# First-group transposes on TensorE, and the DRAM round trip split into a write and a later read, both on SyncE

## The chip, the core and the metric

The kernel runs on one core of a Trainium2 chip. Its engines are TensorE (PE: matrix products and transposes by a product with the identity), VectorE (DVE), ScalarE (ACT), GpSimd (POOL) and SyncE (SP, which only issues transfers here). Each engine works through its own instructions in order; an instruction waits until the semaphores of what it needs are reached, and what stands behind it on its engine waits too. The metric is the device time of one execution in microseconds (us), lower is better.

## The reference, cut to what matters

Two models are chained on an input of 256 rows x 1024, all in float32. The first has four layers, each a mixer (retention, conformer convolution, short convolution, retention) and an MLP. The second has two layers of FFN, token mix (RWKV-7, gated linear attention and gated delta net side by side), FFN and a small gated projection (PLE).

```python
def squared_relu_mlp(x, w1, w2):                 # w1 1024x4096, w2 4096x1024
    return jnp.square(jax.nn.relu(x @ w1)) @ w2

def _swiglu(x, w1, w3, w2):                      # w1, w3 1024x2816, w2 2816x1024
    return (jax.nn.silu(x @ w1) * (x @ w3)) @ w2

# first block, per layer i
x = x + rms_norm(mixer(rms_norm(x, g0)), g1)
x = x + rms_norm(squared_relu_mlp(rms_norm(x, g2), mlp_w1[i], mlp_w2[i]), g3)
# second block, per layer i
x = layer_norm(a * x + 0.5 * _swiglu(x, first FFN's weights))
x = layer_norm(a * x + token_mixing(x, ...))
x = layer_norm(a * x + 0.5 * _swiglu(x, second FFN's weights))
x = layer_norm(a * x + sigmoid(x @ ple_w_gate[i]) * (p[i] @ ple_w_proj[i]))
```

In the token mix, the RWKV branch forms a decay from `tanh(w_lo) @ w2`; `tanh(w_lo)` is the tile `tw` below.

## The kernel before

**Products.** Each float32 operand is split into a high and a low part: `t2h`/`t2l` for the activations (cast on ACT, L351; subtraction on DVE, L352), `wh`/`wl` for the weights (L223, L224; the trace prints the low ones as `whl` and `whxl`). `mm3` (L59) then runs three matmuls, high x high, low weight x high, high weight x low, per 128 x 512 tile of the result. A unit is one 128 x 1024 or 128 x 2 x 512 piece of weights: six matmuls per half of the rows.

**Halves.** The 256 rows are two halves of 128, h0 and h1. `drive` walks through a stage's units; h1 uses a unit five units after h0 (`PACE`), so a weight is loaded and split once. Weights are loaded by SP ahead of their use (`load_unit`, L201) into a few buffers `raw` and `rawx`, cast and subtracted some units ahead (`split_unit`), and released when h1 is done.

**MLP and FFN.** `mlp` takes the hidden width of 4096 in eight groups of 512: four `w1` units per group, then relu (ACT) and the square (DVE), then four `w2` units that add into the accumulators `acc`. `ffn` has eleven groups of 256 with four `f1` and two `f2` units, and silu (ACT) and a product `glu` (DVE) between. The order is w1(0), w1(1), w2(0), w1(2), w2(1) and so on, so each group has one w1 group of time between its activation and its use as the left operand.

**The transpose between.** The activation must be transposed to be the left operand. For all groups but the last, `tr_dma` does this without PE: DVE transposes 32 x 32 blocks into `tz` (L369), POOL issues the write of `tz` to a DRAM tile `td` (L371), and SP issues four reads back into `ty` in the other block order (L375), placed behind the last weight load asked for (`issue_after(s.last_load)`). At k == 4 of the next w1 group, `split_late` casts `ty` to `t2h` and subtracts for `t2l`, placed behind the last weight cast. The last group (7 of the MLP, 10 of the FFN) is transposed on PE with the identity (`tr`, L66 in the trace, into `tp`), since no w1 group is left to hide a trip behind.

**What sets the order.** A scheduler orders each engine's instructions from the program, with its own model of durations, and the `issue_after` edges bind it. In the token-mix phases `side_step` weaves the three branches' chains between the units: a chain yields a number, and is continued when the builder's clock has advanced by so much. `H_W` is the number the RWKV chain yields between `tw` and its use (L1215).

Of the kernel before, what the change touches and what calls it, by code (L numbers as in the profile page):

```python
# [28 lines left out]
SIDE_1 = 1.6  # L29
H_L = 8.0  # L30
H_P = 9.0
H_W = 4.0
H_C = 5.0
H_E = 4.0
LATENCY = 3.5
# [15 lines left out]
class Builder:  # L51
# [309 lines left out]
            s.nc.tensor.transpose(tp[:, j, :], src[:, j * 128:(j + 1) * 128], s.ident)  # L361
        return tp

    def tr_dma(s, src, n):


        nc = s.nc
        z = s.B2((128, 4, n, 32), "tz")
        nc.vector.transpose(z, src.rearrange("p (c a j) -> p a c j", a=4, j=32))  # L369
        d = s.dram.tile([128, 4, n * 32], F32, tag=f"td{n}", bufs=4, name="td")  # L370
        nc.gpsimd.dma_start(d, z.rearrange("p a c j -> p a (c j)"))  # L371
        y = s.B2((128, 4, n, 32), "ty")
        with s.tc.issue_after(s.last_load):
            for a in range(4):
                nc.sync.dma_start(y[32 * a:32 * a + 32].rearrange("i b c j -> i b (c j)"),  # L375
                                  d.rearrange("(b i) a x -> a i b x", b=4)[a])
        return y.rearrange("p b c j -> p c b j")

    def split_late(s, src):
# [90 lines left out]
    def mlp(s, h, lhs, rin):  # L470
        nc = s.nc
        out = [s.acc(), s.acc()]
        r = {}

        def w1(g):
            mm = s.mmb()
            for k in range(0, 8, 2):
                W = yield "w1"
                if k == 4 and g:
                    at[g - 1] = [s.split_late(r.pop(g - 1))]  # L480
                for kk in range(2):
                    s.mm3(lhs, k + kk, W, [(mm, kk * 512, 512, k + kk == 0, k + kk == 7)])
            a = s.B2(name="relu")
            nc.scalar.activation(a, mm, AF.Relu, scale=rin)
            a2 = s.B2(name="relu2")
            nc.vector.tensor_tensor(a2, a, a, op=ALU.mult)

            r[g] = s.tr_dma(a2, 4) if g < 7 else a2

        at = {}  # L490
        yield from w1(0)
        for g in range(8):
            if g < 7:
                yield from w1(g + 1)
            for k in range(4):
                W = yield "w2"
                if g == 6 and k == 1:
                    at[7] = [s.tr_split(r.pop(7))]
                s.mm3(at[g], k, W, [(out[c], c * 512, 512, g == 0 and k == 0, g == 7 and k == 3) for c in range(2)])
        return out  # L500

# [370 lines left out]
    def ffn(s, h, lhs):  # L872
        nc = s.nc
        out = [s.acc(), s.acc()]
        r = {}

        def w1(g):
            mm = s.mmb()
            for k in range(0, 8, 2):
                W = yield "f1"  # L880
                if k == 4 and g:
                    at[g - 1] = [s.split_late(r.pop(g - 1))]
                for kk in range(2):
                    s.mm3(lhs, k + kk, W, [(mm, kk * 512, 512, k + kk == 0, k + kk == 7)])
            a = s.B2((128, 256), "silu")
            nc.scalar.activation(a, mm[:, 0:256], AF.Silu)
            b = s.B2((128, 256), "glu")
            nc.vector.tensor_tensor(b, a, mm[:, 256:512], op=ALU.mult)
            r[g] = s.tr_dma(b, 2) if g < 10 else b

        at = {}
        yield from w1(0)
        for g in range(11):
            if g < 10:
                yield from w1(g + 1)
            for k in range(2):
                W = yield "f2"
                if g == 9 and k == 1:
                    at[10] = [s.split(s.tr(r.pop(10), 2)[:, 0:2, :])]
                s.mm3(at[g], k, W, [(out[c], c * 512, 512, g == 0 and k == 0, g == 10 and k == 1) for c in range(2)])  # L900
        return out

# [268 lines left out]
    def rwkv(s, h, i, q):  # L1171
# [24 lines left out]
        def need(name):  # L1196
            if (name, i, h) not in sh:
                yield name, i, h
            if h and name != "lo" and ("halo", name, i) not in sh:
                yield "halo", name, i  # L1200
            return sh[name, i, h]
# [12 lines left out]
        k = yield from need("rk")  # L1214
        yield H_W  # L1215
        pw, pa = s.mmb((128, 4, 128)), s.mmb((128, 4, 128))
# [679 lines left out]
```

## Time and profile before

| what | value |
|---|---|
| three runs | 3037.0, 3037.02, 3039.89 us, median 3037.02 |
| profiled execution | 3039.6 us, span of the core 3037.8 us, mean granted TensorE clock 0.987 |
| busy, share of the span | PE 96%, PE weight loads 77%, DVE 66%, ACT 50%, POOL 10% |
| transfers | 548.95 MB, 181 GB/s on average |

The stages lie in this order in the span (us, rounded, from the timeline): retention to 223, MLP to 409, conformer to 547, MLP to 735, short convolution to 830, MLP to 1010, retention to 1218, MLP to 1400; then FFN to 1600, mix to 1976, FFN to 2180, PLE to 2208, FFN to 2417, mix to 2795, FFN to 3000, PLE to the end.

In the rows below, a timeline row has the start, the duration, the engine, the line, the operation and `output<-input`, and in brackets how long the engine was idle before it and what released it. A row of waits has the total, the number and the longest. A row of issues has the number, KB each and the median us from issue to landing. A row of windows has for each engine the busy time and (instructions), then the granted clock, the busy share of the DMA engines and GB/s. Matmuls are pipelined: their starts tell the pace, their ends are modelled.

### The profile page before, as it was taken

The page shows a single profiled execution, that of the slowest core. Times are in us where ns is not written, and L with a number is a line of the kernel's source. Part 1 is how long each engine was busy: PE and PEld are TensorE (multiplying, and loading weights), DVE is VectorE, ACT ScalarE, POOL GpSimd, SP SyncE. Part 2 cuts the span into 40 slices and gives each one's busy share as a digit, 9 for nine tenths or more (in the row PEclk, how much of TensorE's full clock was granted, in tenths as well). Part 3 has the DMA queues.
Part 4 walks back from the last instruction along what each step waited for, and adds up shares of the span by engine and source line. Part 5 has one row for each costly group of instructions (what it writes and reads, how often), then busy time and mean ns, then how long its engine had stood idle before and what let it go on. Part 6 is the DMA issues. An engine that isn't in the chain of part 4 may idle for free. (4 is left out here: it accounts for less than half of the span.)

```text
span 3037.8 us, 49444 instructions
## 1 busy us (share of the span) xinstructions
PE 2922.3 (96%) x18650; PEld 2342.2 (77%) x18650; DVE 1993.3 (66%) x3175; ACT 1522.0 (50%) x2348; POOL 289.1 (10%) x488
## 2 busy tenths in 40 slices
PE   8999998999999999999999999989999999999998
PEld 6777877788778878787877777868777777777786
DVE  7566678666766756665567766665665676667556
ACT  4454554555544535544447664444444486654443
POOL 0000024100000000120001000000011100000000
PEclk9999999999999999999999999999999999999999
DMA  7466752576677645786766233477667643335673
GB/s 237 154 186 225 245 160 71 184 251 209 187 237 242 191 155 179 230 262 196 221 187 176 79 112 106 132 218 230 197 196 224 179 131 100 104 112 155 210 234 123
DMA packets 342991, 548.95 MB, mean 181 GB/s; under 512 B 76757, under 2 KB 205985, under 8 KB 342752
## 3 DMA queue, kind: packets, MB, share of 16 engines
q1 hardware_dynamic: 325760, 496.02, 53.3%
q0 software_dynamic: 16416, 47.67, 4.7%
q8 instruction: 147, 2.41, 0.3%
q10 hardware_dynamic: 576, 2.10, 0.2%
q14 instruction: 92, 0.75, 0.1%
HBM read 519.45 MB, written 26.21 MB: 180 GB/s over the span
## 5 line engine op out<-in xcount | busy, mean ns | idle before, releaser
L59 PE MATMUL acc<-wh,t2h 128*128 128x512 f32 (+1 forms) x1512 | 618.5, 409 | 37.4 <-ACT t2h L351 35.7
L59 PE MATMUL acc<-whl,t2h 128*128 128x512 f32 (+1 forms) x1512 | 597.9, 396 | 0.4 <-DVE whl L224 0.4
L224 DVE TENSOR_TENSOR whl<-raw,wh 128x1024 fp32r<-128x1024 f32 x341 | 414.7, 1218 | 250.1 <-ACT wh L223 244.1
L223 ACT CAST wh<-raw 128x1024 fp32r<-128x1024 f32 x341 | 356.8, 1046 | 392.5 <-PE acc L59 259.7
L59 PE MATMUL acc<-wh,t2l 128*128 128x512 f32 (+1 forms) x1512 | 511.6, 395 | 3.1 <-DVE t2l L352 3.1
L224 DVE TENSOR_TENSOR whxl<-raw,whx 128x1024 fp32r<-128x1024 f32 x272 | 329.8, 1214 | 224.5 <-ACT whx L223 220.0
L223 ACT CAST whx<-raw 128x1024 fp32r<-128x1024 f32 x272 | 284.4, 1047 | 300.5 <-PE acc L59 136.8
L59 PEld LDWEIGHTS acc<-wh,t2h 128*128 128x128 f32 x1512 | 287.7, 190 | 115.4 <-ACT t2h L351 49.0
L59 PE MATMUL acc<-whx,t2h 128*128 128x512 f32 (+1 forms) x856 | 348.2, 407 | 4.7 <-ACT t2h L351 4.5
L59 PE MATMUL acc<-whxl,t2h 128*128 128x512 f32 (+1 forms) x856 | 339.1, 396 | 0.0
L59 PEld LDWEIGHTS acc<-wh,t2l 128*128 128x128 f32 x1512 | 285.8, 190 | 67.7 <-DVE t2l L352 6.7
L59 PEld LDWEIGHTS acc<-whl,t2h 128*128 128x128 f32 x1512 | 287.8, 190 | 54.6 <-issue 1.0
L59 PE MATMUL mm<-whx,t2h 128*128 128x512 f32 x800 | 312.9, 392 | 5.9 <-ACT whx L223 5.3
L59 PE MATMUL mm<-whx,t2l 128*128 128x512 f32 x800 | 311.6, 390 | 0.7 <-DVE t2l L352 0.7
L59 PE MATMUL mm<-whxl,t2h 128*128 128x512 f32 x800 | 311.8, 390 | 0.4 <-DVE whxl L224 0.4
L59 PE MATMUL acc<-whx,t2l 128*128 128x512 f32 (+1 forms) x856 | 285.4, 395 | 5.4 <-DVE t2l L352 5.3
L224 DVE TENSOR_TENSOR whxl<-rawx,whx 128x1024 fp32r<-128x1024 f32 x142 | 173.1, 1220 | 126.7 <-ACT whx L223 123.5
L224 DVE TENSOR_TENSOR whl<-rawx,wh 128x1024 fp32r<-128x1024 f32 x145 | 177.2, 1223 | 118.7 <-ACT wh L223 112.1
L223 ACT CAST wh<-rawx 128x1024 fp32r<-128x1024 f32 x145 | 152.4, 1051 | 162.2 <-PE acc L59 106.9
L223 ACT CAST whx<-rawx 128x1024 fp32r<-128x1024 f32 x142 | 148.8, 1049 | 167.5 <-PE mm L59 90.4
L59 PEld LDWEIGHTS acc<-whx,t2h 128*128 128x128 f32 x856 | 163.1, 191 | 43.5 <-ACT t2h L351 7.5
L59 PEld LDWEIGHTS acc<-whx,t2l 128*128 128x128 f32 x856 | 162.8, 191 | 42.0 <-DVE t2l L352 7.0
(618 smaller groups left out, 4190.8 us busy)
## 6 DMA issues: line engine op xcount, KB each, us to landing
raw<-in_mlp_w SPq DMA_DIRECT2D x153, 512.0 KB, 4.6
raw<-in_w_in SPq DMA_DIRECT2D x128, 512.0 KB, 3.6
raw<-in_ffn_w SPq DMA_DIRECT2D x216, 256.0 KB, 3.8
rawx<-in_mlp_w SPq DMA_DIRECT2D x103, 512.0 KB, 4.6
rawx<-in_ffn_w SPq DMA_DIRECT2D x136, 256.0 KB, 3.9
raw<-in_ret_w_in SPq DMA_DIRECT2D x58, 512.0 KB, 4.1
raw<-in_ffn_w SPq DMA_DIRECT2D x53, 512.0 KB, 4.5
rawx<-in_ret_w_in SPq DMA_DIRECT2D x38, 512.0 KB, 4.3
```

The lines of the kernel that those rows point to most:

```text
L59: r = m0(out, a, b, **k)
L223: c = nc.scalar.copy(wh[:, 0:n], r[:, 0:n])
L224: nc.vector.tensor_tensor(wl[:, 0:n], r[:, 0:n], wh[:, 0:n].bitcast(F32), op=ALU.subtract)
```

## The change

It has four parts. Group 0 of every MLP and FFN is transposed on PE, at k == 4 of w1(1). For the other groups but the last, `tr_dma` is split: `tr_out` does the DVE transpose and issues the write to DRAM, now on SP behind the last weight load asked for, and `tr_in` issues the four reads, written at k == 1 of the previous group's second projection, again behind the last weight load then. POOL issues none of these writes any more. And `H_W` goes from 4 to 8.

```diff
-H_W = 4.0
+H_W = 8.0
...
-    def tr_dma(s, src, n):
+    def tr_out(s, src, n):
         nc = s.nc
         z = s.B2((128, 4, n, 32), "tz")
         nc.vector.transpose(z, src.rearrange("p (c a j) -> p a c j", a=4, j=32))
         d = s.dram.tile([128, 4, n * 32], F32, tag=f"td{n}", bufs=4, name="td")
-        nc.gpsimd.dma_start(d, z.rearrange("p a c j -> p a (c j)"))
+        with s.tc.issue_after(s.last_load):
+            nc.sync.dma_start(d, z.rearrange("p a c j -> p a (c j)"))
+        return d, n
+
+    def tr_in(s, dn):
+        d, n = dn
         y = s.B2((128, 4, n, 32), "ty")
         with s.tc.issue_after(s.last_load):
             for a in range(4):
-                nc.sync.dma_start(y[32 * a:32 * a + 32].rearrange("i b c j -> i b (c j)"),
-                                  d.rearrange("(b i) a x -> a i b x", b=4)[a])
+                s.nc.sync.dma_start(y[32 * a:32 * a + 32].rearrange("i b c j -> i b (c j)"),
+                                    d.rearrange("(b i) a x -> a i b x", b=4)[a])
         return y.rearrange("p b c j -> p c b j")
...
     def mlp(s, h, lhs, rin):
-                if k == 4 and g:
+                if k == 4 and g > 1:
                     at[g - 1] = [s.split_late(r.pop(g - 1))]
+                if k == 4 and g == 1:
+                    at[0] = [s.tr_split(r.pop(0))]
...
-            r[g] = s.tr_dma(a2, 4) if g < 7 else a2
+            r[g] = s.tr_out(a2, 4) if 0 < g < 7 else a2
...
                 if g == 6 and k == 1:
                     at[7] = [s.tr_split(r.pop(7))]
+                elif g < 6 and k == 1:
+                    r[g + 1] = s.tr_in(r[g + 1])
...
     def ffn(s, h, lhs):
-                if k == 4 and g:
+                if k == 4 and g > 1:
                     at[g - 1] = [s.split_late(r.pop(g - 1))]
+                if k == 4 and g == 1:
+                    at[0] = [s.split(s.tr(r.pop(0), 2)[:, 0:2, :])]
...
-            r[g] = s.tr_dma(b, 2) if g < 10 else b
+            r[g] = s.tr_out(b, 2) if 0 < g < 10 else b
...
                 if g == 9 and k == 1:
                     at[10] = [s.split(s.tr(r.pop(10), 2)[:, 0:2, :])]
+                elif g < 9 and k == 1:
+                    r[g + 1] = s.tr_in(r[g + 1])
```

How this moves instructions, at three places.

**SP in the first FFN.** `in_ffn_w_2` are weight loads, `td` the write to DRAM (L372 in the changed kernel), `ty` the reads (L375 before, L382 in the changed kernel). Before:

```order
L201 DMA raw<-in_ffn_w_2 128x2x256 x2
L375 DMA ty<-td 32x4x64 x4
L201 DMA raw<-in_ffn_w_2 128x2x256 x2
L201 DMA raw<-in_ffn_w_2 128x1024
L201 DMA rawx<-in_ffn_w_2 128x1024
L201 DMA rawx<-in_ffn_w_2 128x2x256
L375 DMA ty<-td 32x4x64 x4
```

In the changed kernel:

```order
L201 DMA raw<-in_ffn_w_2 128x1024
L372 DMA td<-tz 128x256
L201 DMA rawx<-in_ffn_w_2 128x1024
L201 DMA rawx<-in_ffn_w_2 128x2x256 x2
L382 DMA ty<-td 32x4x64 x4
L201 DMA raw<-in_ffn_w_2 128x2x256 x6
L372 DMA td<-tz 128x256
L201 DMA rawx<-in_ffn_w_2 128x1024
L372 DMA td<-tz 128x256
L201 DMA rawx<-in_ffn_w_2 128x1024
L382 DMA ty<-td 32x4x64 x4
```

Each write now stands in SP's order, and between it and its own reads stand some weight loads (none to three of them, or the other half's write). In the MLPs it is a write, two loads, the reads, then again. The sequence of the 1124 weight loads themselves is the same in both.

**PE in the first MLP, group 0 of h0.** `mm` is the first projection, `acc` the second. Before, the second projection begins:

```order
L59 MATMUL mm<-whl,t2h 128x512
L59 MATMUL mm<-wh,t2l 128x512
L59 MATMUL acc<-wh,t2h 128x512
L59 MATMUL acc<-whl,t2h 128x512
L59 MATMUL acc<-wh,t2h 128x512
```

In the changed kernel the transposes come first, 21 matmuls of the first projection follow, and then the second begins as before:

```order
L59 MATMUL mm<-wh,t2h 128x512
L59 MATMUL mm<-whl,t2h 128x512
L59 MATMUL mm<-wh,t2l 128x512
L66 MATMUL tp<-ident,relu_1941 128x128 x4
L59 MATMUL mm<-whx,t2h 128x512
L59 MATMUL mm<-whxl,t2h 128x512
```

The 16 first groups bring 8 x 4 transposes in the MLPs and 8 x 2 in the FFNs; the DRAM round trips go from 136 to 120.

**PE in the first mix.** `lo` is the input of the RWKV chain's short vectors, whose transposes lead to `tw`; `w2a` are the small weights applied to `tw`. Before, 24 matmuls with weights stand between the transposes of h0's `lo` and the first use of `tw`, the last of them here:

```order
L59 MATMUL acc<-wh,t2h 128x512
L59 MATMUL acc<-whl,t2h 128x512
L59 MATMUL acc<-wh,t2l 128x512
L59 MATMUL mm<-tw,w2a_10927 128x128 x4
L59 MATMUL tp<-shd,w2a_10927 128x128 x4
```

In the changed kernel there are 42, and the other half's `lo` is transposed before them:

```order
L66 MATMUL mm<-ident,lo 128x128 x2
L66 MATMUL mm<-ident,lo 32x128
L59 MATMUL acc<-wh,t2h 128x512
L59 MATMUL acc<-whl,t2h 128x512
L59 MATMUL acc<-wh,t2l 128x512
L59 MATMUL acc<-wh,t2h 128x512
L59 MATMUL acc<-whl,t2h 128x512
L59 MATMUL acc<-wh,t2l 128x512
L59 MATMUL tp<-tw,w2a_10890 128x128 x4
```

The steps that follow in the chain, and the other two branches' steps woven among them, take other places in both mixes as a result.

## The prediction

> **What bounds the kernel now.** I read the page's busy rows first, then PE's waits, then the timeline at the longest of them.
>
> ```profile
> PE 2922.3 (96%) x18650; PEld 2342.2 (77%) x18650; DVE 1993.3 (66%) x3175; ACT 1522.0 (50%) x2348; POOL 289.1 (10%) x488
> PE acc L59 <- ACT t2h L351: 40.2, 27, 3.4
> PE acc L59 <- DVE t2l L352: 8.4, 7, 2.6
> L59 PE MATMUL acc<-wh,t2h 128*128 128x512 f32 x1496 | 613.7, 410 | 37.4 <-ACT t2h L351 35.7 <-DVE rb L563 1.0 <-ACT sg L616 0.5
> ```
>
> TensorE (PE) sets the end: 2922 of the 3037.8 us span. An edit gains only what lies in PE's remaining 115 us, or in a slow PE clock. The largest single wait there is the second projection (accumulator `acc`) waiting for ScalarE's cast `t2h` of the transposed activation: 40.2 us in 27 waits (columns: total, times, longest). One of them, in the first MLP's first group:
>
> ```profile
> 232.72 0.71 DVE L369 STREAM_TRANSPOSE tz<-relu 128x512 f32<-128x512 f32 x1
> 233.72 0.55 POOL L371 DMA_DIRECT2D td<-tz  x1 [0.81 <-DVE tz L369]
> 238.32 1.75 SPq L375 DMA_DIRECT2D ty<-td  x4
> 241.96 0.62 ACT L351 CAST t2h<-ty 128x512 fp32r<-128x512 f32 x1 [2.17 <-DMA ty<-td]
> 240.31 0.39 PE L59 MATMUL mm<-wh,t2l 128*128 128x512 f32 x1
> 242.63 0.50 PE L59 MATMUL acc<-wh,t2h 128*128 128x512 f32 x1 [1.93 <-ACT t2h L351]
> 242.96 0.39 PE L59 MATMUL acc<-whl,t2h 128*128 128x512 f32 x1
> 243.19 0.39 PE L59 MATMUL acc<-wh,t2h 128*128 128x512 f32 x1
> ```
>
> Start, duration, engine; in brackets the idle time and its releaser. DVE's block transpose starts at 232.72, the write and read-back through DRAM last until 241.96, and PE stands for 1.93. Matmuls otherwise start 0.227 apart, so the first one's 0.33 and the modelled end (0.39 against 0.227) add 0.27 to each stall. The trip takes about 9 us; the first group has the work of one group to hide it, every later group more.
>
> Long stalls also slow what follows:
>
> ```profile
> 2017.81 0.79 PE L59 MATMUL acc<-wh,t2h 128*128 128x512 f32 x1 [3.04 <-ACT t2h L351]
> 2023.94 0.40 PE L59 MATMUL acc<-wh,t2h 128*128 128x512 f32 x1
> 2017.10:2023.90 6.80, 6.09 (x14) 4.79 (x15) 2.77 (x5) 2.04 (x4) 0.54 (x1) 0.50 0.53 185
> 2024.00:2031.00 7.00, 7.00 (x32) 5.58 (x31) 3.23 (x4) 2.68 (x4) 0.54 (x1) 1.00 0.64 187
> 262.60:266.10 3.50, 3.50 (x10) 2.68 (x10) 1.88 (x4) 1.08 (x2) 0.54 (x1) 0.51 0.22 80
> 569.80:576.70 6.90, 6.25 (x15) 4.90 (x16) 4.16 (x5) 3.18 (x4) 0.58 (x1) 0.51 0.74 258
> 2232.10:2239.00 6.90, 6.08 (x14) 4.84 (x15) 1.96 (x6) 0.97 (x3) 1.09 (x2) 0.51 0.92 290
> 2836.30:2843.10 6.80, 5.64 (x13) 4.46 (x14) 2.76 (x5) 2.04 (x4) 0.54 (x1) 0.50 0.64 213
> ```
>
> In the window rows the third number from the end is the granted clock. After the 3.04 us stall it is 0.50 for about 7 us, and 14 matmuls take 6.13 us instead of 3.2.
>
> **The change, part by part.**
>
> *Term A, first groups go to PE.* There are 16 first groups (8 stages, two halves); 13 stall: 1.93, 2.17, 3.17, 1.17, 1.15, 0.85 and 1.46 in the four MLPs, 2.32, 1.73, 3.04, 3.19, 1.67 and 3.39 in the FFNs. Sum 27.2. Restarts: 13 x 0.27 = 3.5. Five of them are followed by a half-clock window (the rows above): 6.13 - 14 x 0.227 - 0.27 = 2.7 for the one shown, 11.7 for the five together with each's own rows. After the change the trip to DRAM is gone there, and in the new order PE has 21 or more matmuls (4.8 us) between the transposes and their use, against 1.3 us for cast and subtraction. A = 42.4 gained; nothing else is late at these places, since weights are cast before PE asks for them there.
>
> *Term B, the transposes on PE.* Last groups already do it:
>
> ```profile
> 379.12 0.62 PE L59 MATMUL acc<-wh,t2l 128*128 128x512 f32 x2
> 379.58 0.60 PE L66 MATMUL tp<-ident,relu 128*128 128x128 f32 x4
> 379.94 0.48 PE L59 MATMUL acc<-wh,t2h 128*128 128x512 f32 x1
> 380.25 0.40 PE L59 MATMUL acc<-whl,t2h 128*128 128x512 f32 x1
> PE tp L66 <- DVE glu L888: 1.0, 2, 0.7
> ```
>
> Four transposes hold the stream 0.36, and the next step is 0.31 instead of 0.227: 0.45. Two cost about 0.24. MLPs 8 x 0.45, FFNs 8 x 0.24: 5.5 lost. Existing ones wait little for their input (1.0 us, twice); up to 0.7 for each of 16, 11 us, is the upper bound.
>
> *Term C, H_W.* Its longer wait moves side-chain work in both mix phases:
>
> ```profile
> PE tp L59 <- ACT tw L1213: 3.5, 1, 3.5
> PE mm L59 <- ACT tw L1213: 1.8, 1, 1.8
> PE mm L59 <- DVE yn L607: 2.1, 6, 0.6
> PE tp L66 <- DVE x L924: 4.4, 5, 2.4
> ```
>
> In before, PE runs 24 weight matmuls (5.4 us) between the chain's transposes and the use of `tw`, and stands 1.8 and 3.5 us; now 42 matmuls (9.5 us) stand there. Gone: 5.3, restarts 0.5 and 0.8 of a half clock after the longer one: 6.6. But everything behind it in the chain moves too, and in the new order a few dependent steps of the other chains stand with nothing between. The trace has no row for them; the nearest are short side waits (`yn`, 0.6 at most) and 2.4 at most for `x`. Bounds: from no new wait (+6.6) to eight of 1.5 (-5.4). I take +4, because most distances stay long, and -1.5 for the last small stage, where a transpose now follows its layer norm more closely.
>
> *Term D, the write leaves POOL.*
>
> ```profile
> L371 POOL DMA_DIRECT2D td<-tz x136 | 74.0, 544 | 1111.5 <-DVE tz L369 1065.5 <-DVE whl L224 17.2 <-issue 13.4
> 2306.41 0.45 DVE L369 STREAM_TRANSPOSE tz<-glu 128x256 f32<-128x256 f32 x1
> 2312.97 0.56 POOL L371 DMA_DIRECT2D td<-tz  x1
> 2322.35 0.50 PE L59 MATMUL acc<-wh,t2h 128*128 128x512 f32 x1 [2.77 <-ACT t2h L351]
> ```
>
> POOL mostly idles for `tz`, so its 74 us are worth nothing. But in the third FFN one write queues 6.1 us behind parameter loads on POOL, and PE later stands 2.77. On SP it does not: +3.0 with the restart.
>
> *Term E, writes and reads in SP's queue.* The nearest rows (issues with KB and median us to landing; the extremes are `ty`'s), and the tightest later group:
>
> ```profile
> SPq L375 <- DMA td<-tz: 303.8, 123, 8.8
> td<-tz POOLq DMA_DIRECT2D x80, 128.0 KB, 3.6
> ty<-td SPq DMA_DIRECT2D x320, 32.0 KB, 2.2
> rawx<-in_ffn_w SPq DMA_DIRECT2D x136, 256.0 KB, 3.9
> DMA to landing us min/median/max: 1.6/2.2/7.3
> 1493.92 0.45 DVE L369 STREAM_TRANSPOSE tz<-glu 128x256 f32<-128x256 f32 x1
> 1497.95 2.89 SPq L375 DMA_DIRECT2D ty<-td  x4
> 1502.32 0.41 ACT L351 CAST t2h<-ty 128x256 fp32r<-128x256 f32 x1 [1.69 <-DMA ty<-td]
> 1504.81 0.39 PE L59 MATMUL acc<-whx,t2h 128*128 128x512 f32 x1
> ```
>
> The write now waits on SP for `tz`, with weight loads queued behind; but SP already stood 303.8 us for `td` in before and the weights never came late, and the new wait ends sooner. Then come one or two loads and the four reads. The trace shows no `td` on SP. Lower bound: the 2.2 of a small read there; upper: the 3.9 of a load. I take 2.5, nearer the read, since 128 KB is small. Trip after `tz`, with L for the landing: 0.3 + L + 0.9 (two loads) + 1.75 (four issues) + 2.2 = 5.2 + L, so 7.7, against 1502.3 - 1494.4 = 7.9 from `tz`'s end to the cast here. This group's PE use came 2.1 us after its cast, in most 3 to 5. Cost: nothing while L is under about 4.8, plus 1 us for one late group at the end of the third FFN, where a long load run precedes the write.
>
> The Trainium skill, "DMA: Bandwidth & Descriptors", section "Queues, rings and completion order", says that on each DMA engine the descriptors of one issuing row are consumed in ring order, and that rows are served round-robin. By that a write on SP's row lands behind the loads ahead of it, where POOL's row let it pass. That speaks against the change; no row here shows it, and it would make L that of a load.
>
> **Sum**: 42.4 - 5.5 + 4 - 1.5 + 3.0 - 1 = 41.4. The profiled execution's own time was 3039.6, so 2998.2 for one like it; it lies 2.6 above the runs' median of 3037.0, from which the sum gives 2995.6. I predict **2996 us**.
>
> **Rivals.**
>
> 1. *The half clock is not the stalls' doing.* It also appears elsewhere, and of two stalls of about 2 us one (2.17) is followed by it and one (1.93) not. If the windows merely move to the next pause, 11.7 is not gained: 3008. Against it: all five follow a stall over 2 us within a microsecond. By the Trainium skill, "TensorE: Matmul & The Clock Gate", Part 1, half rate comes after an idle window of about 3.4 us; none of these stalls is that long, yet the granted clock fell, so the rows already go beyond the rule.
>
> 2. *Side chains pay for H_W.* New waits at Term C's lower bound: 9.4 less than I take, and as much again if the chains end the phase late: 3005 to 3015.
>
> 3. *The new transposes wait for their input*, so that the change does not do what it says. 16 x 0.7 = 11: 3007. Against: the row of `glu`, two waits only.
>
> 4. *FFN reads come late, some.* L near 5.5: the 36 first-half groups lose about 0.5 each with restart: 3014.
>
> 5. *Slower side: the same place, L of 7.* Weight loads saturate the queue and each write lands behind two of them. Then the trip is 12.2, 4.3 more than in before; less the usual slack of 3, plus 0.27, each of the 36 groups stalls 1.6: 57 lost, 3053. It decides from about 4.8 and eats the whole gain near 6.4. For it: a read took 7.3 at worst, and the DMA share (second number from the end in the window rows) is 0.92 in one FFN window. Against: medians of 3.6 and 2.2, and shares of 0.53 and 0.64 in two others.
>
> **How the numbers follow.** Forecast (2988 to 3002): 0.60. Rival 1: 0.08, 2: 0.10, 3: 0.06, 4: 0.09, 5: 0.07. This kernel's runs cannot tell less than 0.2% (6 us) from no change. Forecast and rivals 1 to 3 are faster (0.84), 4 mostly (0.05 of 0.09); no change 0.05; slower 0.06. The range leaves out rival 5 and part of 2 and of 4: 2985 to 3016.
>
> **What would show it.** Right: PE's wait on `t2h` falls from 40 us to under 8 and its first-group places vanish from the timeline; windows of 0.5 clock at the five stages are gone; `tp<-ident,relu` doubles to 64 and PE busy rises by about 3 to 5 less the clock's 12; `tw` leaves PE's waits; `td` on SP lands in 2 to 3 us and PE shows no wait for `t2h` in FFN groups 1 to 9. Wrong: `td` landing above 4.8 us, PE waiting for `ty` through the FFNs, casts `wh` waiting for `raw`, or new side waits in the mix phases.

## The result, and the profile after

| kernel | runs | median us | ratio to before, 95% interval |
|---|---|---|---|
| before | 3035.63 to 3039.89 | 3037.01 | |
| after | 2991.6 to 2998.18 | 2993.52 | 0.9858 [0.9841, 0.9875] |

The changed kernel is faster by 1.4%. Its profiled execution took 2998.18 us with a span of 2996.4, so it is 41.4 shorter than that of before (3037.8). First the page's busy row, PE's wait for `t2h`, the transposes by tile, and the issues with their median time to landing:

```profile
PE 2914.0 (97%) x18698; PEld 2341.8 (78%) x18698; DVE 1983.5 (66%) x3159; ACT 1522.3 (51%) x2348; POOL 213.1 (7%) x352
PE acc L59 <- ACT t2h L351: 9.9, 12, 2.2
L66 PE MATMUL tp<-ident,relu 128*128 128x128 f32 x64 | 9.6, 272 | 0.0
L66 PE MATMUL tp<-ident,glu 128*128 128x128 f32 x32 | 6.1, 273 | 0.3 <-DVE glu L901 0.3
td<-tz SPq DMA_DIRECT2D x48, 256.0 KB, 3.2
ty<-td SPq DMA_DIRECT2D x192, 64.0 KB, 5.1
td<-tz SPq DMA_DIRECT2D x72, 128.0 KB, 2.4
ty<-td SPq DMA_DIRECT2D x288, 32.0 KB, 2.9
```

PE's wait for `t2h` fell from 40.2 us in 27 waits to 9.9 in 12; no first group is among them. The two longest, 2.25 and 2.02 us in the conformer, stood in before at the same length.

The write lands 2.4 us (FFN) and 3.2 us (MLP) after its issue on SP, sooner than the 3.6 and 3.7 that it took on POOL. The reads take longer: 5.1 in the MLPs, 2.9 in the FFNs, against 2.3 and 2.2 in before.

What a first group's transposes now cost is seen in the timeline of the first MLP. Starts lie 0.23 apart, but 0.36 and 0.32 around the four transposes:

```profile
237.06 0.60 PE L66 MATMUL tp<-ident,relu 128*128 128x128 f32 x4
237.42 0.48 PE L59 MATMUL mm<-whx,t2h 128*128 128x512 f32 x1
237.74 0.39 PE L59 MATMUL mm<-whxl,t2h 128*128 128x512 f32 x1
```

Two whole stages in windows, the first MLP and the second FFN, first in before, then in after (the length stands behind the bounds, the granted clock third from the end):

```profile
232.20:407.00 174.80, 170.70 (x753) 140.14 (x752) 107.95 (x117) 87.92 (x107) 11.46 (x21) 0.99 0.70 226
1987.00:2165.20 178.20, 173.42 (x751) 140.62 (x750) 102.91 (x131) 78.88 (x107) 11.11 (x21) 0.98 0.73 223
```

```profile
233.80:403.40 169.60, 169.59 (x760) 140.04 (x759) 106.60 (x115) 88.06 (x107) 3.88 (x7) 1.00 0.78 227
1971.20:2145.90 174.70, 173.19 (x761) 140.26 (x759) 104.19 (x131) 80.64 (x110) 0.72 (x2) 1.00 0.77 228
```

The MLP is now busy from end to end (169.59 of 169.60) at full clock. The FFN has its full clock back too, but keeps 1.5 us of idle PE: not all is right there.

Where the 41.4 lie (us from the first transpose on PE of a stage to that of the next, profiled executions; the token mixes begin with their second half's, the PLEs count with the FFN ahead of them, the last one to its last matmul):

| stages | before | after | gain |
|---|---|---|---|
| MLP 1 to 4 | 185.5, 186.1, 181.6, 183.4 | 180.3, 180.6, 179.8, 179.7 | 5.2, 5.5, 1.8, 3.8: 16.2 |
| FFN 1 to 4 | 200.6, 232.0, 209.2, 231.3 | 197.3, 222.8, 202.9, 223.3 | 3.3, 9.2, 6.3, 8.0: 26.8 |
| token mix 1 and 2 | 375.4, 378.3 | 378.5, 375.7 | -3.1, 2.7: -0.4 |
| all else | | | -1.3, of it -2.0 in the first retention |

The 2.0 of the first retention are not the change's: a stretch at half clock stands there at 22 us, which the changed kernel's other profiled execution, after_again below, doesn't have (211.8 us there, 211.2 in before, 213.2 here).

### The profile page after: what moved, and what is told of

The parts are those of the page before. It is cut to its first block, busy times and chain, and to the rows that moved or that the text cites. A ratio compares the mean times of both kernels' runs of the same rounds, so it can differ in the third digit from the quotient of the medians.

```text
span 2996.4 us, 49205 instructions
## 1 busy us (share of the span) xinstructions
PE 2914.0 (97%) x18698; PEld 2341.8 (78%) x18698; DVE 1983.5 (66%) x3159; ACT 1522.3 (51%) x2348; POOL 213.1 (7%) x352
## 5 line engine op out<-in xcount | busy, mean ns | idle before, releaser
L59 PE MATMUL acc<-wh,t2h 128*128 128x512 f32 (+1 forms) x1512 | 611.6, 405 | 10.9 <-ACT t2h L351 8.5
```

The costliest lines, as they stand in the source:

```text
L59: r = m0(out, a, b, **k)
```

## The gain that nobody asked for, and the loss

Two places in the FFNs go otherwise than the prediction has it; both are a matter of one engine's order, and the experiments below turn on them.

**At the end of the second and fourth FFN** (the ones ahead of a PLE) PE waits for the last subtraction. VectorE's and PE's timeline there in before, with a window behind the pause, and then in after:

```profile
2179.91 1.41 DVE L922 SCALAR_TENSOR_TENSOR z<-z,mv,v 128x512 f32<-128x512 f32 x2
2181.24 1.41 DVE L924 SCALAR_TENSOR_TENSOR x<-z,rstd,v 128x512 f32<-128x512 f32 x2
2182.56 1.29 DVE L352 TENSOR_TENSOR t2l<-tp,t2h 128x512 fp32r<-128x512 f32 x2
2183.30 0.73 PE L59 MATMUL acc<-whx,t2l 128*128 128x512 f32 x2 [2.65 <-DVE t2l L352]
2183.00:2191.00 8.00, 7.70 (x27) 6.20 (x28) 3.12 (x4) 0.00 (x0) 0.48 (x1) 0.79 0.88 294
```

```profile
2159.72 0.64 DVE L352 TENSOR_TENSOR t2l<-tp,t2h 128x512 fp32r<-128x512 f32 x1
2160.34 1.41 DVE L937 SCALAR_TENSOR_TENSOR z<-z,mv,v 128x512 f32<-128x512 f32 x2
2160.42 0.74 PE L59 MATMUL acc<-whx,t2l 128*128 128x512 f32 x2 [0.31 <-DVE var L644]
```

In before the subtraction stood behind four operations of the layer norm; in after it stands ahead of them. PE's pause fell from 2.65 to 0.31, and the half-clock stretch behind it (0.79 on average over 8 us, that is 3.4 us at half, which costs 1.6) is gone. That is 2.65 - 0.31 + 1.6 = 3.9 us, and 7.9 with the fourth FFN's, where 2.65 became 0.34. Nothing in the diff names these instructions; the scheduler put them in another order once the stage's work had changed.

**In the later groups of each FFN** some casts of the transposed activation come late. ScalarE in after, first half of the first FFN, group 8, with the reads' row (four of the five are this group's; the reads issued from 1527.7 to 1529.1 land at most 3.3 later) and what PE does:

```profile
L382 SPq DMA_DIRECT2D ty<-td x5: 376/430/432, 1527.2 to 1529.1; - x5
DMA to landing us min/median/max: 1.7/2.0/3.3
1535.90 1.05 ACT L223 CAST wh<-raw 128x1024 fp32r<-128x1024 f32 x1 [1.66 <-PE acc L59]
1536.86 0.40 ACT L351 CAST t2h<-ty 128x256 fp32r<-128x256 f32 x1
1536.56 0.61 PE L59 MATMUL acc<-wh,t2l 128*128 128x512 f32 x2
1537.30 0.50 PE L59 MATMUL acc<-wh,t2h 128*128 128x512 f32 x1
1537.64 0.40 PE L59 MATMUL acc<-whl,t2h 128*128 128x512 f32 x1
1538.60 0.73 PE L59 MATMUL acc<-wh,t2l 128*128 128x512 f32 x2
```

The data are there by 1532.4. The cast starts at 1536.86, because it stands behind a weight cast that waits 1.66 us for PE to give its buffer free. PE then starts `acc<-wh,t2h` 0.29 late, and its `t2l` 0.27 late. Groups 7, 8 and 9 of the first half do so in all four FFNs: 3 x 2 x 0.27 = 1.6 us each, 6.4 in all. To this comes a restart: the matmul behind each late one starts 0.34 after it instead of 0.227 (1537.64 here), 0.11 more. With it the 24 stalls cost 24 x 0.38 = 9.2 us.

## The experiments

No kernel leaves out any of the computation; one, said below, adds work. All medians are compared with runs of before on the same chip.

### One part alone, one part undone

Group 0 on PE and nothing else of the change (writes on POOL, reads at once, `H_W` 4):

```diff
-                if k == 4 and g:
+                if k == 4 and g > 1:
                     at[g - 1] = [s.split_late(r.pop(g - 1))]
+                if k == 4 and g == 1:
+                    at[0] = [s.tr_split(r.pop(0))]
...
-            r[g] = s.tr_dma(a2, 4) if g < 7 else a2
+            r[g] = s.tr_dma(a2, 4) if 0 < g < 7 else a2
```

> The kernel before with one part of the change: group 0 of each MLP and FFN transposed on PE; all other groups by the old trip (POOL write, reads at once), H_W 4. Theory (the first groups carry the gain): 27.2 of stalls, 3.5 of restarts and 11.7 of half clock go, 5.5 of transposes come: 37 less than before, 3000 us (2995 to 3005), and the wait of the second projection on the cast falls from 40 us to under 15. Rival (the write on SP and the later reads carry a large part): above 3015. Rival (the half clock stays and only the gaps are won): about 3011, with windows of clock 0.5 elsewhere.

2996.75 us, ratio 0.9857 [0.984, 0.9874]: as fast as the whole change. Two stalls that the change also removes are still there, in the fourth MLP and the third FFN. Both come from POOL's order, in opposite ways:

```profile
PE acc L59 <- ACT t2h L351: 14.4, 16, 2.2
1285.81 1.07 POOL L978 DMA_DIRECT2D gm<-in_c_gmask  x2
1292.96 0.43 DVE L979 CAST gmask<-gm 128x512 uint8<-128x512 f32 x1 [2.92 <-DMA gm<-in_c_gmask]
1294.04 0.72 PE L59 MATMUL acc<-wh,t2l 128*128 128x512 f32 x2 [2.72 <-DVE t2l L352]
2289.19 0.50 PE L59 MATMUL acc<-wh,t2h 128*128 128x512 f32 x1 [2.18 <-ACT t2h L351]
```

In the third FFN a write stands behind parameter loads on POOL, as Term D has it. In the fourth MLP it is the other way round. POOL stood 14.28 us for a transpose until it could issue a write at 1284.74, and asked for the parameter `gm` only behind it. VectorE waits 2.92 for `gm`, to cast it, and the subtraction `t2l` that PE needs stands behind that cast (1293.30). In before the same cast waits 1.89; in after, where POOL has none of these writes, the loads of `gm` were issued over 30 us ahead of their casts, and nothing waits.

The write on SP and the later read for groups 1 on, with group 0 left as it was and `H_W` 4 (against after; the MLP's lines, the FFN's are alike):

```diff
-                    at[0] = [s.tr_split(r.pop(0))]
+                    at[0] = [s.split_late(r.pop(0))]
...
-            r[g] = s.tr_out(a2, 4) if 0 < g < 7 else a2
+            r[g] = s.tr_out(a2, 4) if 0 < g < 7 else a2 if g else s.tr_dma(a2, 4)
```

> The kernel before with the other part: writes on SP and reads asked for later for groups 1 and up, while group 0 keeps the old trip by POOL with reads at once; H_W 4. Theory: the first-group stalls stay, one stall of 2.8 us in the third FFN and one of 1.7 in the fourth MLP (POOL's queue behind parameter loads) go, and small stalls of 0.3 per cast come late in the FFNs: 3036 us (3030 to 3042). Rival (the queue carries the gain): 3015 or less. Rival (reads late): 3045 or more, with PE waiting for the cast in FFN groups 1 to 9.

3027.4 us, ratio 0.9958 [0.9944, 0.9971]: faster than expected. The first groups still stall, the longest 3.55 in the third FFN, but their stalls sum to 15.1 us here and to 27.2 in before; PE's wait for `t2h` is 25.2 us in 22 waits, 15 less than before's 40.2, and the order at the FFN ends came out as in after.

`H_W` alone, in before and out of after:

```diff
-H_W = 4.0        # before_hw8
+H_W = 8.0
...
-H_W = 8.0        # after_hw4
+H_W = 4.0
```

> The kernel before with H_W at 8 and nothing else. By the prediction's Term C: the two waits on tw (1.8 and 3.5 us) go, 4 us are won: 3033. By the trace of the changed kernel (first mix 3.1 longer, second 2.7 shorter): within 2 us of before, 3037. Rival (side chains pay for it): 3040 or more, with new side waits in both mix phases.

> The changed kernel with H_W back at 4. If H_W is worth 4 us (Term C): 2997.5. If it is worth nothing: 2993.5 within 2, with the waits on tw back and other side waits gone. If H_W costs: 2990 or less.

Before with 8: 3035.82, ratio 0.9986 [0.9974, 0.9999]. After with 4: 2993.57, ratio 0.9852 [0.9836, 0.9869], like after itself. The waits on `tw` do come back with 4 (here after with 4), and cost nothing that shows:

```profile
PE tp L59 <- ACT tw L1228: 2.2, 1, 2.2
PE mm L59 <- ACT tw L1228: 1.6, 1, 1.6
```

Over the fourteen profiled executions of this study the two mixes together took 752.5 us on average with 4 (five of them, 750.1 to 755.6) and 750.9 with 8 (nine, 746.9 to 754.7); one kernel profiled twice (after, after_again) differs by 3.3 in the first mix alone. A microsecond or two of `H_W` can't be told in this.

The four numbers don't add: 41.3 (the gain of group 0 alone, 3038.04 - 2996.75), 10.6 (SP's part alone) and 2.2 (`H_W` alone) make 54, and all together give 43.5. Two things come with either of the first two and can be had once only: the FFN ends' 7.9, and some 12 of the first groups' stalls (27.2 - 15.1). That is more than the 10.6 missing; what offsets the rest the runs don't part.

### Is the half clock the stalls' doing?

Before, with eight extra matmuls (1.8 us, into a tile that nothing reads) ahead of the waiting matmul at the five first groups that a half-clock stretch follows:

```diff
+    def filler(s, lhs, W):
+        tp = s.tpb((128, 512))
+        for _ in range(8):
+            s.nc.tensor.matmul(tp, lhs[0][0][:, 0, :], W[0][:, 0:512], start=True, stop=True)
...
+                if fill and g == 0 and k == 0:
+                    s.filler(lhs, W)
```

> The kernel before with eight extra matmuls (1.8 us, into a PSUM tile that nobody reads) ahead of the second projection's first use at the five first groups whose stall was followed by a half clock: the trip stays as long, but PE is not idle. If idle time of over 2 us brings the half clock: the five windows go and with them some 10 us, the order shifting a little: 3028 (3024 to 3032). Rival 1 (the half clock has another cause): 3037 or more, windows still there.

3042.66 us, ratio 1.0014 [1.0003, 1.0025]: not won. Three of the five pauses fell below 2 us and lost their half clock. In the second and fourth FFN the scheduler put only part of the extra work ahead of the pause; those pauses stayed long and kept theirs. One of each kind, in the second MLP and in the second FFN, the stalled matmul and the window behind it:

```profile
568.52 0.50 PE L59 MATMUL acc<-wh,t2h 128*128 128x512 f32 x1 [1.95 <-ACT t2h L351]
568.00:576.00 8.00, 7.48 (x33) 6.17 (x34) 6.34 (x8) 4.70 (x6) 1.01 (x2) 1.00 0.64 218
2018.53 0.79 PE L59 MATMUL acc<-wh,t2h 128*128 128x512 f32 x1 [3.46 <-ACT t2h L351]
2018.00:2026.00 8.00, 7.47 (x26) 6.04 (x27) 3.24 (x6) 3.37 (x6) 0.54 (x1) 0.79 0.39 123
```

The extra 5 x 1.8 = 9 us and stretches at other pauses ate the gain, so the total says nothing. What does say something is the count over the traces of all fourteen kernels and executions: of PE's pauses in between (without the first 25 us and the last stage), how many were followed within about a microsecond by a stretch at 0.50?

| pause of PE, us | with half clock behind it |
|---|---|
| 1.0 to 2.0 | 1 of 104 |
| 2.0 to 2.5 | 40 of 85 |
| 2.5 to 3.0 | 27 of 33 |
| 3.0 and more | 14 of 17 |

The longer the pause, the likelier the half clock, and below 2 us there is next to none. Rival 1 falls for the first groups.

Why only half of the pauses of 2 to 2.5 us? In each trace the stretches start on one grid of 3.413 us and last one, two or three of its windows (those at the very end of a span, up to 11 us, apart). Sorted by the idle time of PE within one such window, the scatter goes. Of the windows at full clock, over the same stretch of the fourteen traces, those with 2.0 us of idle time or more are followed by one at 0.50 in 81 of 81 cases, those with 1.5 to 2.0 in 13 of 46, those with less in 27 of 11 750. A pause of 3.09 us in before (at 1984) falls into two windows, as 1.90 and 1.20, and brings none. Of the 27, 22 lie in the token mixes, in windows with almost no idle time among many small matmuls; their cause is open.

The Trainium skill, "TensorE: Matmul & The Clock Gate", Part 1, gives a free-running window of 3413 ns, and the lengths agree with it; its idle time of a whole window before the clock falls doesn't, since 2.0 us within a window are enough.

### What do SP's writes cost in the FFNs?

Can the late reads do without the write on SP? The changed kernel with the writes back on POOL:

```diff
-        with s.tc.issue_after(s.last_load):
-            nc.sync.dma_start(d, z.rearrange("p a c j -> p a (c j)"))
+        nc.gpsimd.dma_start(d, z.rearrange("p a c j -> p a (c j)"))
```

> The changed kernel with the writes of groups 1 and up back on POOL; the reads stay late, the rest as changed. It parts the queue of the write from the time of the reads. Theory (the queue matters only where POOL is behind parameter loads): Term D's stall in the third FFN comes back, 3 us, and the wait of 1.7 in the fourth MLP: 2998 (2995 to 3001). Rival (the late reads alone make room): 2993.5 within 2. Rival (a write on SP is itself dearer): 2991 or less.

2982.74 us, ratio 0.9813 [0.9801, 0.9826]: 11 faster than the change, against the theory and as the last rival has it. The fourth MLP's stall did not come back (180.25 us, 179.66 in after); one of the two loads of `gm` is asked for ahead of the write here. The stall of the third FFN is back, and longer: its write is held behind some twenty parameter loads on POOL for 10 us. VectorE's transpose, POOL's write and PE there:

```profile
2262.48 0.45 DVE L369 STREAM_TRANSPOSE tz<-glu 128x256 f32<-128x256 f32 x1
2272.92 0.55 POOL L371 DMA_DIRECT2D td<-tz  x1 [0.61 <-DMA mu<-in_rw_mu]
2282.31 0.50 PE L59 MATMUL acc<-wh,t2h 128*128 128x512 f32 x1 [4.10 <-ACT t2h L351]
```

So the write on SP, meant for all groups, helps one group of one FFN and costs more elsewhere. The late reads, on the other hand, help: this kernel differs from the one with group 0 on PE alone by them and `H_W`, and is some 13 us faster (ratios 0.9813 and 0.9857). Of the 16.1 between the two spans 7.0 lie in the FFNs and 4.0 in the fourth MLP.

Where SP's write costs: ScalarE in the first FFN of this kernel, group 8 again.

```profile
1528.63 1.05 ACT L223 CAST wh<-rawx 128x1024 fp32r<-128x1024 f32 x1 [1.36 <-PE mm L59]
1529.58 0.40 ACT L351 CAST t2h<-ty 128x256 fp32r<-128x256 f32 x1
1533.87 0.39 PE L59 MATMUL acc<-wh,t2h 128*128 128x512 f32 x1
```

The cast stands one weight cast earlier, and PE uses it 3.9 us after its end. From VectorE's transpose to the landing of the reads it took 7.9 us here and 8.3 in after (medians of the FFNs' groups), but from there to the start of the cast 1.3 and 2.0, in the first half alone 1.3 and 3.1: the data come at nearly the same time, the cast does not.

The stalls are small, yet many. In the second FFN with its PLE 33 matmuls of after start 0.02 to 2 us later than 0.227 behind the one ahead, 5.8 us in all. In the last kernel of this section, pool_mixed, with POOL writes there, it is 15 and 1.6 us. The difference of 4.2 is nearly the whole of the stage's 222.8 - 218.3 = 4.5. Of after's 5.8, 2.3 are the six stalls of groups 7 to 9; most of the rest lies behind them, at the end of the FFN.

### Earlier reads, a second group on PE

Reads asked for at once behind SP's write, not a group later:

```diff
-            r[g] = s.tr_out(a2, 4) if 0 < g < 7 else a2
+            r[g] = s.tr_in(s.tr_out(a2, 4)) if 0 < g < 7 else a2
...
-                elif g < 6 and k == 1:
-                    r[g + 1] = s.tr_in(r[g + 1])
```

> The changed kernel with the reads asked for at once, right behind the write on SP, as the kernel before did with POOL's. Theory: the 24 small stalls of 0.27 in the FFNs (first half, groups 7 to 9), 6.4 us together, come from reads asked for late, which puts the cast later in ScalarE's order; with early reads they go: 2988 (2985 to 2991). Rival (SP standing for the write makes weights late): 2996 or more, with weight casts waiting for loads.

3020.65 us, ratio 0.9937 [0.9925, 0.995]: 27 slower than the change, so the theory falls. The reads land sooner (from the transpose to the landing 6.8), but a cast `t2h` now stands behind two weight casts, the first of which waits for PE. Its data had landed at 1503.86:

```profile
1503.35 1.05 ACT L223 CAST whx<-rawx 128x1024 fp32r<-128x1024 f32 x1 [1.67 <-PE acc L59]
1504.70 1.04 ACT L223 CAST whx<-raw 128x1024 fp32r<-128x1024 f32 x1 [0.30 <-DMA raw<-in_ffn_w]
1505.66 0.40 ACT L351 CAST t2h<-ty 128x256 fp32r<-128x256 f32 x1
1506.11 0.50 PE L59 MATMUL acc<-whx,t2h 128*128 128x512 f32 x1 [1.44 <-ACT t2h L351]
```

PE's wait for `t2h` in the FFNs grows from 2.6 us in after to 21.3. The rival's number came, its sign did not: SP stands 106.1 us for `td` (32.5 in after), yet the weight casts of the FFNs wait 15.5 us for their loads, and 15.6 in after. With the write on SP the early read costs 27 us here, and what the trace shows at the small stalls is ScalarE's order again.

Group 1 on PE as well (the MLP's lines; group 1's trip to DRAM goes, and the FFN is alike):

```diff
-                if k == 4 and g == 1:
-                    at[0] = [s.tr_split(r.pop(0))]
+                if k == 4 and 0 < g < 3:
+                    at[g - 1] = [s.tr_split(r.pop(g - 1))]
```

> The changed kernel with group 1 transposed on PE as well as group 0, in all eight stages: 48 more transposes in the same form, on groups that had no stall. It measures Term B by itself: 8 x 0.45 + 8 x 0.24 = 5.5, so 2999. If the transposes slip into pauses: 2994. If each waits 0.7 for its input: 3010.

2991.12 us, ratio 0.9837 [0.9824, 0.9849]. Three of the MLPs became 0.95 longer (180.28 to 181.21, 179.79 to 180.72, 179.66 to 180.64): two times 0.48 for four transposes, where the prediction had 0.45. The whole is no dearer all the same: the mixes took 747.0 us in this execution and 754.2 in that of after, a difference that executions of one kernel show too (748.3 in after_again below). So one more group on PE costs an MLP what it should, and no more.

### Is it ScalarE's order?

The changed kernel, with an edge that puts each late cast `t2h` of an FFN ahead of the next weight cast asked for:

```diff
+            if getattr(s, "late", None) is not None:            # in split_unit
+                st.enter_context(s.tc.issue_after(s.late))
+                s.late = None
...
-            return s.split(src)               # in split_late
+            hl = s.split(src)
+        s.late = s.split_ins if src.shape[1] == 2 else None
```

> The changed kernel with one edge more: in the FFNs the next weight cast on ScalarE is issued behind the activation cast t2h that the program names before it. Writes stay on SP, reads stay late. Theory (what the changed kernel loses in the FFNs to writes on POOL comes from ScalarE's order, which puts t2h one weight cast later, not from the landing of the data): the small stalls of the first half's groups 7 to 9 go and with them 2 to 4 us per FFN: 2983 (2980 to 2987). Rival (the write in SP's queue itself costs): 2991 or more, with t2h waiting for ty.

2995.4 us, ratio 0.9848 [0.9828, 0.9869]: nothing won, and the number is the rival's. The edge moved group 8's cast and its stalls went, but groups 7 and 9 still stand behind the same weight cast, and other waits came at the ends of the FFNs. Group 7, and an end:

```profile
1519.57 1.06 ACT L226 CAST whx<-raw 128x1024 fp32r<-128x1024 f32 x1 [4.38 <-PE acc L59]
1520.53 0.40 ACT L354 CAST t2h<-ty 128x256 fp32r<-128x256 f32 x1
2163.54 0.50 PE L59 MATMUL acc<-whx,t2h 128*128 128x512 f32 x1 [2.46 <-ACT t2h L354]
```

The edge binds only what is asked for later; that weight cast had been asked for earlier. ScalarE stood idle for 4.38 us there with the data landed (at 1515.9). But the rival's sign is there too: where the edge does bind, the casts are now asked for ahead of their data, and ScalarE waits 47.5 us for `ty` in the four FFNs, in 31 casts (8.2 in 8 in after). This run alone doesn't decide between the two.

So in a further run the cast itself is asked for one unit earlier in the first half, from group 4 on:

```diff
-                if k == 4 and g > 1:
+                if g > 1 and k == (2 if h == 0 and g > 4 else 4):
                     at[g - 1] = [s.split_late(r.pop(g - 1))]
```

> The changed kernel, in which the FFNs' first half asks for the cast of a late group (group 4 on) one unit earlier, at k == 2 of the next first-projection group; writes and reads stay on SP where they are. Theory (the casts are late because ScalarE has them behind a weight cast that waits for PE, while the data has landed: in the changed kernel the first half's casts stand 2.9 to 5.3 us after the landing): the two stalls of 0.25 to 0.29 per late group go (6 in each FFN, 6.4 us in all), and about 2.4 at the ends of two FFNs may go with them: 2985 to 2988. Rival (the write's place on SP makes the reads late, and the cast's place is not the cause): the casts now wait on ScalarE for ty, weight casts queue behind them, and the stalls stay or grow: 2992 or more.

2985.94 us, ratio 0.9828 [0.9808, 0.9849]: within the theory's 2985 to 2988, with writes and reads on SP as in after. But the way there is another than expected. The scheduler now puts the second half's cast beside the first half's, and one small stall stays in each of six groups instead of two in each of three, here group 7's:

```profile
1516.79 1.05 ACT L223 CAST wh<-rawx 128x1024 fp32r<-128x1024 f32 x1 [1.67 <-PE mm L59]
1517.75 0.71 ACT L351 CAST t2h<-ty 128x256 fp32r<-128x256 f32 x2
1518.20 0.50 PE L59 MATMUL acc<-wh,t2h 128*128 128x512 f32 x1
```

With the restart 6 x 0.36 = 2.2 us in an FFN, and it was 2.3. What went are waits at the FFN ends: the second, third and fourth FFN took 220.6, 201.7 and 220.0 against 222.8, 202.9 and 223.3. The number was met, the mechanism was not; and of the 14.1 by which the profiled span is shorter than after's, 7.3 lie in the token mixes, which differ nearly as much between executions of one kernel. All four FFNs together took 846.3 us in after, 840.6 here, and 830.3 in pool_mixed below. So the order of the casts alone, with every transfer where the change has it, moves the FFNs by some 6 of these 16 us. That the data were there when the casts were late is shown by the landings. Counted by matmuls that start late, 9 of the 16 are the 24 stalls of groups 7 to 9 with their restarts, and some 6 lie at the ends of the second, third and fourth FFN. No run here removes the stalls with the writes on SP, so whether an order exists in which these cost nothing stays open.

### A version that beats both

Writes on POOL as in after_pool, and on SP only for the one group that POOL's parameter loads hold up, group 5 of the third FFN:

```diff
+        if sp:
+            with s.tc.issue_after(s.last_load):
+                nc.sync.dma_start(d, z.rearrange("p a c j -> p a (c j)"))
+        else:
+            nc.gpsimd.dma_start(d, z.rearrange("p a c j -> p a (c j)"))
...
+            r[g] = s.tr_out(b, 2, third and g == 5) if 0 < g < 10 else b
```

> Writes on POOL with late reads, as in the run with POOL's writes, except group 5 of the third FFN, whose two writes go on SP, past POOL's parameter loads. That run still had one stall there of 4.1 us with 0.3 of restart and 1.6 of half clock: 6 less than it, 2977 (2974 to 2980). Rival (the two writes on SP shift ScalarE's order in that FFN as in the changed kernel): 2980 or more, with stalls of 0.1 there.

2978.1 us, ratio 0.9798 [0.9779, 0.9816], as expected. The changed kernel on the same chip:

> The changed kernel itself, on the same chip as the other two, so that they can be compared with it: 2993.5 within 3.

2992.34 us, ratio 0.9845 [0.9825, 0.9864]. The mixed kernel is 14 faster than the change. The third FFN in windows, in after_pool and here:

```profile
2185.50:2363.90 178.40, 173.64 (x759) 141.75 (x760) 103.40 (x134) 78.06 (x105) 22.55 (x43) 0.99 0.71 211
```

```profile
2189.00:2361.00 172.00, 171.38 (x761) 141.09 (x762) 103.85 (x135) 78.31 (x105) 21.70 (x41) 1.00 0.74 220
```

The stage takes 6.4 less: the stall of 4.10, its restart of 0.27 and the half clock's 1.6 make 6.0 of it.

## Why the prediction was right, point by point

The sum was 41.4 and the profiled spans differ by 41.4; the median came out at 2993.5 for a predicted 2996. The agreement to the decimal is luck: single terms were off by up to 8 us and cancelled, and by the medians the gain is 43.5, since the profiled execution of after was the slowest of its four.

- **Term A, first groups, right.** All thirteen stalls are gone, with their restarts and the five half-clock stretches. The MLPs show it unmixed: of terms A and B 5.3, 5.1, 2.0 and 2.0 were due, and 5.2, 5.5, 1.8 and 3.8 came.
- **Term B, transposes on PE, right.** 0.45 was taken for four; 0.48 was measured by adding a group. Rival 3 (they wait for input) did not happen: 0.0 and 0.3 us of idle time stand in the rows of `tp`, and PE's busy time fell by 8.3, as foretold (3 to 5 more, less the clock's 12).
- **Term C, `H_W`, not borne out.** The net 2.5 was not seen in the changed kernel. The two waits on `tw` vanish as foretold, but the mixes lost 0.4 in sum, and `H_W` set back to 4 leaves the time as it is; in before, 8 gained 2.2. This is the mild end of rival 2: short waits elsewhere (some of them 1.3 to 1.4 us without any releaser in the trace, as at 1680 and 1689 in the first mix) take their place. What these are stays open. The first mix also holds a stretch at half clock, 6.83 us from 1800.4, that cost 2.5 and is absent in after_again.
- **Term D, POOL's queue, right in kind and too small.** The third FFN's stall went; one more, 1.69 us in the fourth MLP, had been overlooked. There it was not a write that queued behind parameter loads, but a parameter load behind a write, with VectorE's `t2l` behind the cast of that parameter. It is the 1.8 by which that MLP did better.
- **Term E, SP's queue, mis-sized.** The landing L was taken at 2.5 and measured at 2.4 in the FFNs, so rivals 4 and 5, which needed 5.5 and 7, did not happen. The error was the step from there to "nothing while L is under about 4.8". It follows the data to their landing (8.3 after the transpose, 7.7 by the sum) and takes the cast to come then; but the cast has a place in ScalarE's order, and that place moved back. The cost was 9.2 by the stalls of groups 7 to 9, where 1 was taken (and the FFNs are 16 dearer than in the best kernel found). The late reads, which the prediction takes only as a risk, gained some 13 with the writes on POOL (with what `H_W` has in it). By the rule on ring order that spoke against the change ("DMA: Bandwidth & Descriptors", "Queues, rings and completion order", in the Trainium skill) the write should have landed like a load; its 2.4 doesn't show that, while the MLPs' reads, at 5.1 instead of 2.3, do come close to a load's 4.6.
- **Not foreseen: the FFN ends, 7.9.** No term had it. FFNs by the prediction: 24.5; less 8.2 for term E, and 7.9 more, make 24.2; measured 26.8. The other 2.6 are not assigned.

Of the signs named beforehand: `tp<-ident,relu` doubled to 64; `tw` left PE's waits; `td` landed within 2 to 3 us in the FFNs (3.2 in the MLPs); the half-clock stretches at the five stages are gone. The wait on `t2h` is 9.9, not under 8, for the conformer's two were not subtracted; and PE does show short waits for `t2h` in FFN groups 7 to 9, the sign against term E.

## What to carry to other kernels

A short stretch of TensorE work, four transposes at 0.48 us, is cheap where it replaces a pause of 2 us or more, since such a pause costs its length, a restart of 0.27 and, where 2.0 us of it fall into one window of the clock's grid, 1.6 us and more of half clock. When a transfer is moved, follow its data beyond the landing, to the place that the first instruction using them has on its engine. A wait in one group (POOL's parameter loads) is mended in that group: moving all the others as well cost 14 us here.

## What the runs showed of the hardware that was not expected

- The granted clock falls to 0.50 after pauses of TensorE from about 2 us, not only from 3: 40 of 85 between 2.0 and 2.5 us, 1 of 104 between 1 and 2. What decides is the idle time within one window of a grid of 3.413 us: from 2.0 us on, half clock followed in 81 of 81 cases. Where the grid lies differs from execution to execution, so one and the same pause can be followed by half clock in one and not in the next.
- Reads on SP's queue, with two weight loads between their write and them, landed in 5.1 us in the MLPs instead of 2.3 (64 KB each), while writes from the same queue landed in 2.4 (128 KB) and 3.2 us (256 KB), no slower than from POOL (3.6 and 3.7 in before).
- Two executions of the changed kernel differ by 3.3 us in the first token mix (378.5 and 375.2). 2.5 of it are a stretch at half clock that only one of them has (6.83 us from 1800.4, with almost no idle time ahead of it); the rest lies mainly in three pauses among its small matmuls that show no releaser (3.6 us in sum, and 2.8).
